# RWKV-7 mixer on one Trainium2 core: four pairs' small products on the array's column tiles, sample states on its four quarters, states loaded at once

## The chip, the cores and the metric

The kernel runs on one core of one Trainium2 chip. The metric is the device time of one execution in microseconds (us); before the change the median of three runs is 1444.45 us (1440.34 to 1446.25). The engines are named as in the profile: PE is TensorE's matrix products, DVE is VectorE, ACT is ScalarE, POOL is GpSimd, SP is SyncE.

## The reference

Two layers of a trunk for a prompt of 256 tokens and eight samples of four new tokens each, 288 columns in all, with D_MODEL 1024. Each layer is a half-step SwiGLU FFN, a mixer, and a second FFN, each after an RMSNorm with shift, scale and gate from a conditioning vector. The mixer is RWKV-7 (8 heads of 64) beside causal pooling; the change is in the RWKV part alone.

```
def _wkv_step(S, inp):
    r_t, w_t, k_t, v_t, a_t, b_t = inp
    sa = jnp.einsum('bhvk,bhk->bhv', S, a_t)
    S = S * w_t[:, :, None, :] + sa[..., None] * b_t[:, :, None, :] + v_t[..., None] * k_t[:, :, None, :]
    y = jnp.einsum('bhvk,bhk->bhv', S, r_t)
    return S, y
...
    kk = kk / jnp.maximum(jnp.sqrt(jnp.sum(kk * kk, axis=-1, keepdims=True)), 1e-12)
    k = hs(k.astype(f32) * (1 + (a - 1) * k_a.astype(f32)))
    S_T, y = lax.scan(_wkv_step, wkv0.astype(f32),
                      (tm(r), tm(decay), tm(k), tm(v), tm(-kk), tm(kk * a)))
    y = ((y - mean) * lax.rsqrt(var + GN_EPS)).reshape(Bn, L, A_WIDTH)
    y = y * ln_w.astype(f32) + ln_b.astype(f32)
    bonus = jnp.sum(r * k * r_k.astype(f32), axis=-1, keepdims=True) * v
    y = (y + bonus.reshape(Bn, L, A_WIDTH)) * g.astype(f32)
```

The samples start from a state of 64 x 64 per head and sample (`state_wkv`, 1 MB per layer), and the new states are outputs.

## The kernel before

Activations lie with channels on the 128 partitions and the 288 tokens in the free dimension. A pair is two heads on one 128-partition tile (`HP` = 4 pairs, index hp or j; e is the head in it). `halves` are partitions 0 to 63 and 64 to 127, `quarter` the four groups of 32.

**Main products.** All large weights come as one stream, a 512 KB tile at a time on SP's queue. For each 128 x 512 strip ACT rounds a high half `wh` (L225), DVE subtracts it for the low half `wl` (L226), and `mm3` (L251) multiplies three times: (wh, xh), (wh, xl), (wl, xh). The "main product" of this text is one such multiplication, 128 x 128 by 288 columns. The halves have four buffers, the raw tiles three.

**The mixer** (L610) interleaves two streams on PE. `main_ops` is a generator of the mixer's main products (input projections, gates, pool branch). The other stream is the RWKV part, small fp32 products written out in order. `add` puts small items into `queue`, each followed by `WEAVE` = 2 steps of `main_ops`; `fill(n)` pops n entries, with n from the table `PLAN` where none is given. So the order of the instructions on each engine is fixed when the program is built, and each engine runs them in that order; only their waits depend on time. PSUM has three banks for main products (`psmm`), four (`pswk`, from `ps_wk`) that all small products share in turn, and one for the modulation (`psmd`).

**The small stream, in order.** Low-rank products (L801) and, for each j, the sum of squares of the keys (L822), four products into four column tiles of one bank; their root; scaled A, R, B, K; the scores MM (L893); a chain of DVE operations that inverts 16 x 16 blocks to GT and, with L1165 to L1197, 64 x 64 blocks; in between the queue's bonus sums (L966) and the transpositions of A and BK (L905). Then the prompt's chunks (L1257, L1262, L1275, `outputs` L1233/L1237, `transposed` L1244), with the samples woven in from the queue: `smp_state` for each pair (L1034 loads the pair's states on ACT's DMA queue, L1037 multiplies them by the rows of A and R, L1040 masks into `ms` and L1041 reduces), `smp_scores`, `smp_rows`, `smp_x`, `smp_u`, `smp_y`, later `smp_last` for each pair (L1136 loads the states again, L1138 makes `uv` on POOL, L1141 multiplies, DVE adds, POOL scales, SP stores). All state tiles of one pair share one buffer, tag "O0". `group_norm` (L1085) takes DVE, ACT and POOL steps (L1092 to L1100) and ends in `yn`, which `transposed` needs; `out_gate` (L1106) makes the output gate, `gated` (L1126) applies it. At the end `yah` (L509) splits the result for the branch product.

## Time and profile before

| what | value |
|---|---|
| median of three runs | 1444.45 us |
| lowest and highest run | 1440.34, 1446.25 us |
| profiled execution's own time | 1440.62 us |
| its span | 1438.8 us |
| mean granted clock of PE | 0.998 |
| mixer of layer 0 in the span, about | 276 to 449 us |
| mixer of layer 1 in the span, about | 988 to 1164 us |

The span runs from the first to the last instruction of the profiled execution; its own time has 1.8 us around it. Times in the rows are microseconds from the span's start. A product in fp32 whose operands are not transposed through the identity is two passes and stands as two instructions in the trace; the count at a row's end is of passes. A bracket at a row's end is idle time before it and what ended it.

### The profile page before, as it was taken

What the parts mean: (1) busy time and instruction counts of PE and PEld (TensorE: products, weight loads), DVE (VectorE), ACT (ScalarE), POOL (GpSimd) and SP (SyncE); (2) the same over time, 40 slices, a digit from 0 to 9 for tenths busy, and PEclk for the clock granted to TensorE, in tenths of its full rate; (3) what the DMA queues carried; (4) which work ended last, traced back from release to release, by engine and by line L of the source; (5) the groups of instructions that cost most, each with busy time, mean ns of one, the idle gap of its engine ahead of it and who ended that gap; (6) DMA issues with size and microseconds to landing.
All of it is one profiled execution on the core that took longest, in us unless ns stands there. A gap on an engine that the chain in (4) does not pass through costs nothing.

```text
span 1438.8 us, 29985 instructions
## 1 busy us (share of the span) xinstructions
PE 1395.2 (97%) x11872; PEld 1292.8 (90%) x11872; DVE 945.0 (66%) x2061; ACT 725.9 (50%) x1477; POOL 110.8 (8%) x155
## 2 busy tenths in 40 slices
PE   6999999998999999999999999999999999999997
PEld 5989999887788999899999999998787899999997
DVE  4655556898766885455667555669967777755554
ACT  4544444675534664444445445447653356545532
POOL 0000001000022010000211000120001200100012
PEclk9999999999999999999999999999999999999999
DMA  9888864443225676787766745553333357445452
GB/s 367 313 283 298 307 242 157 148 134 125 87 94 158 253 251 226 275 302 264 252 226 234 264 147 163 172 179 124 112 105 109 103 188 268 158 152 171 161 169 100
DMA packets 72573, 281.92 MB, mean 196 GB/s; under 512 B 9584, under 2 KB 11760, under 8 KB 63088
## 3 DMA queue, kind: packets, MB, share of 16 engines
q1 hardware_dynamic: 66384, 272.24, 54.6%
q10 hardware_dynamic: 6048, 7.77, 1.8%
q8 instruction: 93, 1.52, 0.4%
q14 instruction: 48, 0.39, 0.1%
HBM read 275.74 MB, written 4.23 MB: 195 GB/s over the span
## 4 chain that ended last, share of the span: by engine, by line
PE 87%; DVE 6%; DMA 2%; issue 2%; ACT 2%; POOL 1%; POOLq 0%; DVEq 0%; ACTq 0%
PE psmm L251 44%; PE pswk L251 31%; PE psmd L315 4%; DVE wl L226 2%; DMA s<-in_wkv 1%; PE pswk L905 1%; PE pswk L1037 1%; PE pswk L393 1%; ACT wh L225 1%; DVE MM L897 1%; DMA o_wkvs<-s 0%; DVE ul L484 0%; DVE xn L481 0%; PE pswk L1262 0%; DMA cc<-in_c 0%
## 5 line engine op out<-in xcount | busy, mean ns | idle before, releaser
L226 DVE TENSOR_TENSOR wl<-raw,wh 128x512 fp32r<-128x512 f32 x732 | 513.7, 704 | 352.3 <-ACT wh L225 341.2
L225 ACT CAST wh<-raw 128x512 fp32r<-128x512 f32 x732 | 452.6, 620 | 563.9 <-PE psmm L251 290.3
L251 PE MATMUL psmm<-uh,wh 128*128 128x288 f32 x1072 | 321.0, 299 | 1.2 <-ACT uh L492 1.2
L251 PE MATMUL psmm<-uh,wl 128*128 128x288 f32 x1072 | 317.8, 296 | 4.5 <-DVE wl L226 4.5
L251 PE MATMUL psmm<-ul,wh 128*128 128x288 f32 x1072 | 317.6, 296 | 0.6 <-DVE ul L493 0.3
L251 PEld LDWEIGHTS psmm<-uh,wh 128*128 128x128 f32 x1072 | 201.9, 188 | 15.8 <-issue 7.7
L251 PEld LDWEIGHTS psmm<-uh,wl 128*128 128x128 f32 x1072 | 201.7, 188 | 8.7 <-DVE wl L226 5.8
L251 PEld LDWEIGHTS psmm<-ul,wh 128*128 128x128 f32 x1072 | 201.8, 188 | 2.6 <-DVE ul L493 1.2
L251 PE MATMUL pswk<-ul,wh 128*128 128x288 f32 x608 | 179.6, 295 | 0.0
L251 PE MATMUL pswk<-uh,wh 128*128 128x288 f32 x608 | 179.4, 295 | 0.0
L251 PE MATMUL pswk<-uh,wl 128*128 128x288 f32 x608 | 179.4, 295 | 0.0
L251 PEld LDWEIGHTS pswk<-uh,wh 128*128 128x128 f32 x608 | 114.5, 188 | 5.4 <-issue 5.0
L251 PEld LDWEIGHTS pswk<-ul,wh 128*128 128x128 f32 x608 | 114.5, 188 | 0.0
L251 PEld LDWEIGHTS pswk<-uh,wl 128*128 128x128 f32 x608 | 114.4, 188 | 0.0
L251 PE MATMUL pswk<-hl,wh 128*128 128x288 f32 x352 | 104.0, 296 | 0.0
L251 PE MATMUL psmm<-hl,wh 128*128 128x288 f32 x352 | 104.0, 295 | 0.0
L251 PE MATMUL psmm<-hh,wh 128*128 128x288 f32 x352 | 103.9, 295 | 0.0
L251 PE MATMUL psmm<-hh,wl 128*128 128x288 f32 x352 | 103.8, 295 | 0.0
L251 PE MATMUL pswk<-hh,wl 128*128 128x288 f32 x352 | 103.8, 295 | 0.0
L251 PE MATMUL pswk<-hh,wh 128*128 128x288 f32 x352 | 103.4, 294 | 0.0
L315 PE MATMUL psmd<-modw,csilu 128*32 128x512 f32 (+2 forms) x832 | 70.5, 481 | 9.4 <-DMA modw<-in_wmod 9.4
L378 POOL TENSOR_TENSOR sq<-x 128x288 f32<-128x288 f32 x28 | 19.8, 707 | 767.1 <-DVE x L520 767.1
(327 smaller groups left out, 2409.7 us busy)
## 6 DMA issues: line engine op xcount, KB each, us to landing
raw<-in_wflat SPq DMA_DIRECT2D x366, 512.0 KB, 3.4
modw<-in_wmod SPq DMA_DIRECT2D x72, 1024.0 KB, 7.0
s<-in_wkv ACTq DMA_DIRECT2D x16, 256.0 KB, 3.0
o_wkvs<-s SPq DMA_DIRECT2D x8, 256.0 KB, 2.9
x<-in_x SPq DMA_DIRECT2D x1, 1152.0 KB, 5.8
o_y<-yo SPq DMA_DIRECT2D x2, 288.0 KB, 2.5
o_y<-yo ACTq DMA_DIRECT2D x2, 288.0 KB, 2.6
o_pool<-po SPq DMA_DIRECT2D x8, 67.5 KB, 2.3
```

The source lines that it names most:

```text
L225: self.nc.scalar.copy(wh, src)
L226: self.nc.vector.tensor_tensor(out=wl, in0=src, in1=wh.bitcast(F32), op=ALU.subtract)
L251: self.last = self.nc.tensor.matmul(ps, w, x, start=start and n == 0, stop=stop and n == 2)
L315: mm = nc.tensor.matmul(self.mod_ps[32 * q:32 * q + 32, :size], self.csilu[:, k, :], w[:, kk, q, :], start=(k == 0), stop=(k == KD - 1))
L378: nc.gpsimd.tensor_tensor(out=t, in0=x, in1=x, op=ALU.mult)
L393: nc.tensor.matmul(ps[:, i:i + 1], s[:, o:o + P], self.cst("ones"), start=n + i == 0, stop=n == len(self.sums) - 1 and i == 2)
L897: V.tensor_tensor(out=MM[:, 2 * e + i, :, q].rearrange("p h x t -> p h (x t)"), in0=pss[e].rearrange("p (h y) -> p h y", h=HP), in1=maskp, ...
L905: T.transpose(ps[:n, 128 * hp:128 * hp + 128], src(hp), ident)
L1037: T.matmul(ps[halves[e], :], ARs[halves[e], hp].rearrange("p x t -> p (x t)"), s0[halves[e]].rearrange("p b v -> p (b v)"), start=True, st ...
```

## The change

Seven edits, all in the mixer but for the last:

- the four key-square products are issued together, after the four squares have been made (`tj` has four buffers)
- the four bonus products likewise, from four `rkk` tiles made ahead; the four transpositions of A become two queue items (`removal`) ahead of the bonus
- states: one tile `s0` for all four pairs, loaded by one DMA at the mixer's start instead of twice for each pair; `smp_state` and `smp_last` take two pairs at a time, one bank for each, and `smp_last` updates `s0` in place and stores two pairs with one DMA
- `at_` places head e of an odd pair in the other half of the output, so that the two pairs' products lie on four quarters of the array
- scores, rows, value rows and yt go into two banks by the parity of the pair, in the same manner
- the queue's items are regrouped: bonus spread and gate for all four tiles at once, lasts in two items (the three lists of the queue have 7 items each instead of 9, 9 and 11)
- the program sets aside less memory for DMA descriptors (`dynamic_dma_scratch_size`), which leaves room for `s0`

```
         def tj(name):
-            return tl([P, NT], "tj", name, bufs=3)
+            return tl([P, NT], "tj", name, bufs=4)
...
         kps = self.ps_wk()
+        kks = []
         for j in range(HP):
             lora_mm(j)
-            t = tl([P, NT], "tj", "kk2", bufs=3)
-            S.activation(out=t, in_=xk[:, j, :], func=AF.Square, scale=self.par(l, "k_k", j))
-            T.matmul(kps[32 * j:32 * j + 32, :NT], hs, t, start=True, stop=True)
+            kks.append(tj("kk2"))
+            S.activation(out=kks[j], in_=xk[:, j, :], func=AF.Square, scale=self.par(l, "k_k", j))
+            if j == HP - 1:
+                for i, t in enumerate(kks):
+                    T.matmul(kps[32 * i:32 * i + 32, :NT], hs, t, start=True, stop=True)
             fill()
...
+        add(lambda: removal(0), lambda: removal(1))
         add(lambda: bonus())
-        add(*[lambda i=i, q=q: token_major(lambda hp: A[:, hp, 2 * i + q, :], AT[halves[q], i, :]) for i in range(2)
-              for q in range(2)])
         add(*[lambda i=i, q=q: token_major(lambda hp: BK[:, hp, i, 2 * q:2 * q + 2, :], BKT[i][:, q, :])
...
-        def rkk(j):
-            t = tj("rkk")
-            V.tensor_tensor(out=t, in0=xr[:, j, :], in1=xk[:, j, :], op=ALU.mult)
-            return t
+        def removal(i):
+            for q in range(2):
+                token_major(lambda hp: A[:, hp, 2 * i + q, :], AT[halves[q], i, :])
+        rkk = [tj("rkk") for _ in range(HP)]
+        for j in range(HP):
+            V.tensor_tensor(out=rkk[j], in0=xr[:, j, :], in1=xk[:, j, :], op=ALU.mult)
...
             for j in range(HP):
-                T.matmul(ps[32 * j:32 * j + 32, :NT], rks[:, j, :], rkk(j), start=True, stop=True)
+                T.matmul(ps[32 * j:32 * j + 32, :NT], rks[:, j, :], rkk[j], start=True, stop=True)
             S.copy(bsum, ps[:, :NT])
...
         bm = self.cst("bmask").unsqueeze(2).to_broadcast([P, NB, 64])
+        s0 = tl([P, HP, NB, 64], "s0")
+        nc.scalar.dma_start(out=s0, in_=self.io["wkv"][l])
         head_loop = [(hp, e) for hp in range(HP) for e in range(2)]
+        def at_(hp, e):
+            return (e + hp) % 2
         def smp_scores():
-            ps = self.ps_wk()
+            pss = [self.ps_wk() for _ in range(2)]
             for hp, e in head_loop:
-                re = halves[e]
-                T.matmul(ps[re, 64 * hp:64 * hp + 64], BKs[re, hp].rearrange("p x t -> p (x t)"),
+                re, o = halves[e], 64 * (hp // 2)
+                T.matmul(pss[hp % 2][halves[at_(hp, e)], o:o + 64], BKs[re, hp].rearrange("p x t -> p (x t)"),
                          ARs[re, hp].rearrange("p x t -> p (x t)"), start=True, stop=True)
-            masks = self.cst("masks").rearrange("p (x t) -> p x t", x=2).unsqueeze(1).to_broadcast([P, HP, 2, NS])
-            V.tensor_tensor(out=SCs, in0=ps[:, 0:256].rearrange("p (h x t) -> p h x t", h=HP, x=2), in1=masks,
-                            op=ALU.mult)
+            masks = self.cst("masks").rearrange("p (x t) -> p x t", x=2).unsqueeze(1).to_broadcast([P, 2, 2, NS])
+            for k in range(2):
+                V.tensor_tensor(out=SCs[:, k::2], in0=pss[k][:, 0:128].rearrange("p (h x t) -> p h x t", h=2, x=2),
+                                in1=masks, op=ALU.mult)
             G.tensor_copy(Gs, self.cst("id32").unsqueeze(1).to_broadcast([P, HP, NS]))
...
-            ps = self.ps_wk()
+            pss = [self.ps_wk() for _ in range(2)]
             for hp, e in head_loop:
-                re = halves[e]
-                T.matmul(ps[re, 64 * hp:64 * hp + 64], BKs[re, hp].rearrange("p x t -> p (x t)"), ident[re, re],
-                         start=True, stop=True)
-            S.copy(BKTs, ps[:, 0:256].rearrange("p (h k) -> p h k", h=HP))
-            ps = self.ps_wk()
+                re, o = halves[e], 64 * (hp // 2)
+                T.matmul(pss[hp % 2][halves[at_(hp, e)], o:o + 64], BKs[re, hp].rearrange("p x t -> p (x t)"),
+                         ident[re, re], start=True, stop=True)
+            for k in range(2):
+                S.copy(BKTs[:, k::2], pss[k][:, 0:128].rearrange("p (h k) -> p h k", h=2))
+            pss = [self.ps_wk() for _ in range(2)]
             for hp, e in head_loop:
-                T.matmul(ps[quarter[2 * e + 1], 64 * hp:64 * hp + 64], xv[halves[e], hp, TP:],
+                o = 64 * (hp // 2)
+                T.matmul(pss[hp % 2][quarter[2 * at_(hp, e) + 1], o:o + 64], xv[halves[e], hp, TP:],
                          ident[halves[e], halves[e]], start=True, stop=True)
-            for e in range(2):
-                r = quarter[2 * e + 1]
-                S.copy(UVs[r], ps[r, 0:256].rearrange("p (h k) -> p h k", h=HP))
-        def smp_state(hp):
-            s0 = tl([P, NB, 64], "O0", "s0")
-            nc.scalar.dma_start(out=s0, in_=self.io["wkv"][l][:, hp])
-            ps = self.ps_wk()
-            for e in range(2):
-                T.matmul(ps[halves[e], :], ARs[halves[e], hp].rearrange("p x t -> p (x t)"),
-                         s0[halves[e]].rearrange("p b v -> p (b v)"), start=True, stop=True)
-            ms = tl([P, NB, 64], "ms")
-            V.tensor_tensor(out=ms, in0=ps.rearrange("p (b v) -> p b v", b=NB), in1=bm, op=ALU.mult)
-            V.tensor_reduce(out=AS[:, hp, :], in_=ms.rearrange("p b v -> p v b"), axis=AX.X, op=ALU.add)
+            for k in range(2):
+                for e in range(2):
+                    r = quarter[2 * e + 1]
+                    S.copy(UVs[r, k::2], pss[k][r, 0:128].rearrange("p (h k) -> p h k", h=2))
+        def smp_state(hps):
+            pss = [self.ps_wk() for _ in hps]
+            for hp, ps in zip(hps, pss):
+                for e in range(2):
+                    T.matmul(ps[halves[at_(hp, e)], :], ARs[halves[e], hp].rearrange("p x t -> p (x t)"),
+                             s0[halves[e], hp].rearrange("p b v -> p (b v)"), start=True, stop=True)
+            for hp, ps in zip(hps, pss):
+                ms = tl([P, NB, 64], "ms", bufs=2)
+                V.tensor_tensor(out=ms, in0=ps.rearrange("p (b v) -> p b v", b=NB), in1=bm, op=ALU.mult)
+                V.tensor_reduce(out=AS[:, hp, :], in_=ms.rearrange("p b v -> p v b"), axis=AX.X, op=ALU.add)
...
         def smp_yt():
-            ps = self.ps_wk()
+            pss = [self.ps_wk() for _ in range(2)]
             for hp, e in head_loop:
-                r = quarter[e]
-                T.matmul(ps[halves[e], 32 * hp:32 * hp + 32], yn[2][r, 64 * hp:64 * hp + 64], ident[r, r],
+                r, o = quarter[at_(hp, e)], 32 * (hp // 2)
+                T.matmul(pss[hp % 2][halves[e], o:o + 32], yn[2][r, 64 * hp:64 * hp + 64], ident[r, r],
                          start=True, stop=True)
-            gated(slice(TP, NT), ps[:, 0:32 * HP])
+            for k in range(2):
+                gated(slice(TP, NT), pss[k][:, 0:64], slice(k, HP, 2))
...
-            y = ps.rearrange("p (h t) -> p h t", h=js.stop - js.start)
-            tmp = tl([P, 512], "pw", "ygw", bufs=2)[:, :ps.shape[1]].rearrange("p (h t) -> p h t", h=js.stop - js.start)
+            n = len(range(HP)[js])
+            y = ps.rearrange("p (h t) -> p h t", h=n)
+            tmp = tl([P, 512], "pw", "ygw", bufs=2)[:, :ps.shape[1]].rearrange("p (h t) -> p h t", h=n)
             V.tensor_tensor(out=tmp, in0=y, in1=out[1][:, js, t], op=ALU.mult)
...
-        def smp_last(hp):
-            s0 = tl([P, NB, 64], "O0", "s0")
-            nc.scalar.dma_start(out=s0, in_=self.io["wkv"][l][:, hp])
-            uv = tl([P, NB, 64], "ms", "uv")
-            G.tensor_tensor(out=uv, in0=UVs[:, hp, :].unsqueeze(1).to_broadcast([P, NB, 64]), in1=bm, op=ALU.mult)
-            ps = self.ps_wk()
-            for e in range(2):
-                T.matmul(ps[halves[e], :], BKTs[halves[e], hp, :], uv[halves[e]].rearrange("p b v -> p (b v)"),
-                         start=True, stop=True)
-            V.tensor_tensor(out=s0, in0=s0, in1=ps.rearrange("p (b v) -> p b v", b=NB), op=ALU.add)
-            G.tensor_tensor(out=s0, in0=s0, in1=gam[:, hp, NCH:].unsqueeze(2).to_broadcast([P, NB, 64]), op=ALU.mult)
-            nc.sync.dma_start(out=self.io["o_wkvs"][l][:, hp], in_=s0)
-        def state(hp):
-            return lambda: smp_state(hp)
-        def last(hp):
-            return lambda: smp_last(hp)
+        def smp_last(hps):
+            uvs = [tl([P, NB, 64], "ms", "uv", bufs=2) for _ in hps]
+            pss = [self.ps_wk() for _ in hps]
+            for hp, uv in zip(hps, uvs):
+                G.tensor_tensor(out=uv, in0=UVs[:, hp, :].unsqueeze(1).to_broadcast([P, NB, 64]), in1=bm, op=ALU.mult)
+            for hp, uv, ps in zip(hps, uvs, pss):
+                for e in range(2):
+                    r = halves[at_(hp, e)]
+                    T.matmul(ps[halves[e], :], BKTs[r, hp, :], uv[r].rearrange("p b v -> p (b v)"),
+                             start=True, stop=True)
+            for hp, ps in zip(hps, pss):
+                s1 = s0[:, hp]
+                V.tensor_tensor(out=s1, in0=s1, in1=ps.rearrange("p (b v) -> p b v", b=NB), op=ALU.add)
+                G.tensor_tensor(out=s1, in0=s1, in1=gam[:, hp, NCH:].unsqueeze(2).to_broadcast([P, NB, 64]), op=ALU.mult)
+            h0, h1 = hps[0], hps[-1] + 1
+            nc.sync.dma_start(out=self.io["o_wkvs"][l][:, h0:h1], in_=s0[:, h0:h1])
...
             fill(1)
-        add(state(0), state(1), smp_scores, state(2), smp_rows, state(3), smp_x, smp_u, smp_y)
+        add(lambda: smp_state((0, 1)), smp_scores, smp_rows, lambda: smp_state((2, 3)), smp_x, smp_u, smp_y)
...
             if c == 1:
-                add(*[lambda js=js: spread_bonus(js) for js in ((0, 1), (2, 3))],
-                    *[lambda js=js: out_gate(js) for js in ((0, 1), (2, 3))],
-                    lambda: outputs(0), last(0), smp_yt, lambda: transposed(0), last(1), last(2), last(3))
+                add(lambda: spread_bonus(range(HP)), lambda: out_gate(range(HP)), lambda: outputs(0), smp_yt,
+                    lambda: transposed(0), lambda: smp_last((0, 1)), lambda: smp_last((2, 3)))
         V.tensor_tensor(out=Sfin, in0=Sfin, in1=gam[:, :, NCH - 1:NCH].to_broadcast([P, HP, 64]), op=ALU.mult)
...
     arrays = pack(inputs)
-    nc = bacc.Bacc("TRN2", target_bir_lowering=False, num_devices=1)
+    nc = bacc.Bacc("TRN2", target_bir_lowering=False, num_devices=1, dynamic_dma_scratch_size=1024)
     io = {}
```

How it stands on the engines. PE, layer 0, around the second state block before (`s` are state tiles, `ARs`, `BKs` the sample rows):

```order
L251 MATMUL psmm<-uh,wh_4733 128x288
L251 MATMUL psmm<-ul,wh_4733 128x288
L1037 MATMUL pswk<-s_4703,ARs 64x512 x2
L251 MATMUL psmm<-uh,wl_4734 128x288
L999 MATMUL pswk<-ARs,BKs 64x64 x8
L251 MATMUL psmm<-uh,wh_4772 128x288
```

and the same place after, where L1054 is the state product, L1013 the scores and L1035 the rows:

```order
L1275 MATMUL pswk<-X_4493,MM 64x64 x16
L1054 MATMUL pswk<-s_4017,ARs 64x512 x4
L1013 MATMUL pswk<-ARs,BKs 64x64 x8
L251 MATMUL psmm<-ul,wh_4742 128x288
L251 MATMUL psmm<-uh,wl_4743 128x288
L251 MATMUL psmm<-uh,wh_4742 128x288
L251 MATMUL psmm<-ul,wh_4742 128x288
L251 MATMUL psmm<-uh,wl_4743 128x288
L251 MATMUL psmm<-uh,wh_4742 128x288
L1035 MATMUL pswk<-consts,BKs 64x64 x8
```

The scores now follow a block of four state products with no main product between; before, a block of two stood among main products.

DVE, layer 0, from the first masked state product on, before (`pw`, `dd` are the pooling's tiles, `SCs` the scores):

```order
L1040 TENSOR_TENSOR ms<-pswk,consts 128x512
L1041 TENSOR_REDUCE AS<-ms 128x64
L226 TENSOR_TENSOR wl_4853<-raw_4597,wh_4852 128x512
L675 TENSOR_TENSOR pw<-px 128x422
L675 TENSOR_TENSOR pw<-pw 128x420
L675 TENSOR_TENSOR pw<-pw 128x416
L1040 TENSOR_TENSOR ms<-pswk,consts 128x512
L678 SCALAR_TENSOR_TENSOR dd<-pw,px 128x256
L684 SCALAR_TENSOR_TENSOR dd<-pw,px 128x32
L1041 TENSOR_REDUCE AS<-ms 128x64
L681 TENSOR_TENSOR dd<-pw,consts 128x16
L1002 TENSOR_TENSOR SCs<-pswk,consts 128x256
```

and after, where L1058 and L1059 are the mask and the reduction, L1017 evicts the scores:

```order
L1058 TENSOR_TENSOR ms<-pswk,consts 128x512
L1059 TENSOR_REDUCE AS<-ms 128x64
L1058 TENSOR_TENSOR ms<-pswk,consts 128x512
L1017 TENSOR_TENSOR SCs<-pswk,consts 128x2x64
L1059 TENSOR_REDUCE AS<-ms 128x64
L1017 TENSOR_TENSOR SCs<-pswk,consts 128x2x64
L1023 STREAM_SHUFFLE shs_4682<-SCs 128x128
L1026 TENSOR_TENSOR shs_4682<-shs_4682,Gs 128x32x3
L1028 TENSOR_TENSOR Gs<-Gs,shs_4682 128x32x3
L1023 STREAM_SHUFFLE shs_4686<-SCs 128x128
L675 TENSOR_TENSOR pw<-px 128x422
L1026 TENSOR_TENSOR shs_4686<-shs_4686,Gs 128x32x2
```

Two state pairs' operations now stand together, and no weight half (`wl`) among them until much further on.

ACT, layer 0, at the mixer's end before (`yah` is the rounded result, `gA` a gate):

```order
L225 CAST wh_5545<-raw_5428 128x512
L1136 DMA s_5412<-in_wkv 128x512
L509 CAST yah<-xv 128x288
L765 ACTIVATE gA_5453<-psmm,par_84 128x288
L225 CAST wh_5561<-raw_5428 128x512
L509 CAST yah<-xv 128x288 x2
L225 CAST wh_5583<-raw_5491 128x512
L509 CAST yah<-xv 128x288
```

and after:

```order
L1115 ACTIVATE ysq_5365<-yn_5361 128x512
L225 CAST wh_5484<-raw_5309 128x512
L225 CAST wh_5506<-raw_5410 128x512
L225 CAST wh_5522<-raw_5410 128x512
L509 CAST yah<-xv 128x288 x4
L225 CAST wh_5544<-raw_5450 128x512
L225 CAST wh_5560<-raw_5450 128x512
L765 ACTIVATE gA_5465<-psmm,par_84 128x288
```

The load of a state tile that stood ahead of `yah` is gone.

## Rows read from the trace of the kernel before

**Rows 1.** The busy table of the whole span.

```profile
PE 1395.2 (97%) x11872; PEld 1292.8 (90%) x11872; DVE 945.0 (66%) x2061; ACT 725.9 (50%) x1477; POOL 110.8 (8%) x155
```

**Rows 2.** Stretches of layer 0's mixer: length, busy by engine, clock, DMA.

```profile
276.00:355.00 79.00, 72.80 (x532) 63.43 (x530) 76.79 (x228) 55.94 (x127) 1.15 (x3) 1.00 0.39 122
328.00:355.00 27.00, 24.39 (x168) 21.10 (x167) 25.74 (x96) 18.32 (x40) 1.15 (x3) 1.00 0.36 112
355.00:441.00 86.00, 83.49 (x1204) 66.88 (x1205) 58.34 (x129) 33.21 (x70) 17.28 (x19) 1.00 0.29 94
```

**Rows 3.** PE's waits, 282 to 450: in total, times, longest.

```profile
PE pswk L893 <- DVE AR L875: 1.6, 1, 1.6
PE pswk L1037 <- DMA s<-in_wkv: 1.6, 1, 1.6
PE psmm L251 <- DVE wl L226: 1.6, 1, 1.6
...
PE pswk L1165 <- DVE dd L681: 1.1, 1, 1.1
```

**Rows 4.** PE's timeline, column tiles and a state pair: start, duration, instruction.

```profile
102.13 3.64 PE L315 MATMUL psmd<-modw,csilu 128*32 128x512 f32 x32
...
381.17 1.08 PE L1037 MATMUL pswk<-s,ARs 64*64 64x512 f32 x4 [1.57 <-DMA s<-in_wkv]
382.18 0.69 PE L1275 MATMUL pswk<-UV,BKT 128*64 128x64 f32 x16
```

**Rows 5.** PE's timeline around a last and yt.

```profile
421.09 1.07 PE L1141 MATMUL pswk<-uv,BKTs 64*64 64x512 f32 x4
422.10 0.40 PE L251 MATMUL psmm<-ybh,wh 128*128 128x288 f32 x1
422.34 0.30 PE L251 MATMUL psmm<-ybl,wh 128*128 128x288 f32 x1
422.47 0.29 PE L251 MATMUL psmm<-ybh,wl 128*128 128x288 f32 x1
...
423.89 0.65 PE L1078 MATMUL pswk<-consts,yn 32*64 32x32 f32 x16
```

**Rows 6.** PE's timeline, transpositions of BK and of yn.

```profile
363.10 1.09 PE L905 MATMUL pswk<-consts,BK 128*128 128x128 f32 x8
...
429.17 0.66 PE L1244 MATMUL pswk<-consts,yn 128*128 128x128 f32 x4
```

**Rows 7.** DVE's groups, 355 to 441: count, busy, mean ns, idle before.

```profile
L226 DVE TENSOR_TENSOR wl<-raw,wh 128x512 fp32r<-128x512 f32 x22 | 15.6, 710 | 5.1 <-ACT wh L225 3.3 <-ACT O L1188 1.4
L1041 DVE TENSOR_REDUCE AS<-ms 128x64 f32<-128x512 f32 x4 | 4.3, 1066 | 0.0
...
L1040 DVE TENSOR_TENSOR ms<-pswk,consts 128x512 f32<-128x512 f32 x4 | 2.8, 688 | 0.8 <-PE pswk L1037 0.8
```

**Rows 8.** DVE's timeline, neighbours and two group norms.

```profile
380.67 0.68 DVE L226 TENSOR_TENSOR wl<-raw,wh 128x512 fp32r<-128x512 f32 x1
381.27 0.25 DVE L1011 TENSOR_TENSOR shs<-shs,Gs 128x96 f32<-128x96 f32 x1
...
419.41 0.69 DVE L1092 TENSOR_REDUCE gn<-pswk 128x8 f32<-128x512 f32 x1 [0.75 <-PE pswk L1237]
...
426.37 0.69 DVE L1100 TENSOR_TENSOR yn<-yn,gn 128x512 f32<-128x512 f32 x1 [1.49 <-POOL gn L1099]
...
436.11 1.52 DVE L1100 TENSOR_TENSOR yn<-yn,gn 128x512 f32<-128x512 f32 x1 [1.53 <-POOL gn L1099]
```

**Rows 9.** Timeline of POOL and ACT near the mixer's end.

```profile
432.91 1.05 POOL L1138 TENSOR_TENSOR uv<-UVs,consts 128x512 f32<-128x512 f32 x1 [6.57 <-PE pswk L1141]
...
444.56 0.33 ACTq L1136 DMA_DIRECT2D s<-in_wkv  x1
444.94 0.43 ACT L509 CAST yah<-xv 128x288 fp32r<-128x288 f32 x1 [4.38 <-DMA o_wkvs<-s]
```

**Rows 10.** DMA issues of the states: count, size, us to landing.

```profile
s<-in_wkv ACTq DMA_DIRECT2D x16, 256.0 KB, 3.0
```

## The prediction, made before the changed kernel was run

> **What bounds the kernel now.** I read the busy table first, then the mixer's stages as windows, then PE's waits there, and last the timelines of the operations that change. Over the whole span PE is busy 97% and DVE 66% [rows 1]. The clock is full throughout (the last figures but two of [rows 2] read 1.00), so no term below is a clock term. The change touches only the mixer, once per layer, and the mixer isn't one stage. From its start to the transposition of GT, 276 to 355, DVE is busy 45.05 of 46 us and 25.74 of the last 27, PE less [rows 2]: DVE bounds it, and PE's waits there end in DVE (1.6 on AR, 1.1 on dd) [rows 3]. From 355 to 441 it is the other way: PE is busy 83.49 of 86 us, DVE 58.34 [rows 2]. The two large waits behind that are the state's DMA (1.6) and, at the stage's end, a weight half wl (1.6) [rows 3]. I call these parts the front and the back, and price one layer; the second has the same pattern.
>
> **The front is worth nothing.** Packing the four squared-key products, keeping the four bonus products together and moving the removal transpositions ahead all save PE's time where PE waits for DVE. The order gives DVE the same instructions in layer 0's front as before, so what PE saves it waits. I take 0; bounded by the two rows of [rows 3] on AR and dd, it could be 1.1 either way. The state load, now one of 1 MB instead of four of 256 KB [rows 10], stands at the mixer's start on ACT's queue, ahead of the pool history's; it has 90 us until it is needed, so I take 0.
>
> **What PE saves in the back.** Tiles do run at the same time. A full-width pass of 288 columns takes 0.13 [rows 5], and yet 32 passes of 512 columns on four column tiles took 3.64 us, 0.11 each; the two products of a state pair, on two diagonal quarters (four passes of 512), took 1.01 from start to next, 0.25 each [rows 4]. Row tiles and column tiles on all four quarters at once are not in this trace. The bounds for two pairs on four quarters are therefore 1.01 (all at once, as the rows of [rows 4] suggest for either kind) and 2.02 (two diagonals in turn); I take 1.01.
> - States: four blocks of 1.01 become two, −2.0. Lasts: 421.09 to 422.10 is 1.01 too [rows 5], so −2.0.
> - Half of BK's transpositions (eight, 1.0 [rows 6]) move to the front, where DVE hides them: −1.0.
> - Scores, rows, X, u, y and yt have as many products as before. The one for yt takes 0.65 [rows 5]; four tiles instead of two could halve such a block or leave it. I take −0.4 for all six (0 to −1.9).
> - Bonus spread and gates are two items instead of four. A main product follows another after 0.13, but after a small block the first takes 0.24 [rows 5], so a switch costs about 0.1 on either side, 0.2 together. The order keeps nearly as many switches (26 against 27), so I take −0.2.
> - The wait for the state's DMA goes: −1.57. It is in the stage that PE bounds, and no load is issued there any more.
> - The tail: PE waits 1.57 for wl at 448.60, since ACT stood 4.38 us behind the store of a state tile (the issue of the next load, 444.56, sits in ACT's queue and waits until the shared tile is stored) and made its halves late [rows 3, 9]. With no load there, the casts run through: −1.57. The later wait of the same kind costs PE nothing now.
> Together −8.74.
>
> **What comes back as new waits.** All four wk banks are taken in pairs now, and evictions by DVE and ACT stand between. Each of these is an estimate, bounded below by 0 and above by the rows named.
> - L1228 behind the last inversion product, with less before it: 0.4. The nearest row is the 1.1 of a small product on a DVE result [rows 3].
> - The scores' third product needs a bank. Two hold the new state pair, one the running sum; so it waits until DVE has evicted the first state bank, 0.69 [rows 7] plus some 0.2 of start: 0.9. In the order the scores follow the state block with nothing between.
> - The rows' products need the second bank, behind another ms, one reduction and the scores' eviction, 0.69 + 1.07 + 0.36, against six main products (0.78) and the scores: 0.65 (0 to 1.1).
> - u needs Xs, which stands 32 DVE instructions behind the first ms. Four ms and four reductions are 7.0 [rows 7], two wl 1.4, and the 22 others at the mean of the rest of the back (58.34 of 129, less 4 × 0.69, 4 × 1.07 and 22 × 0.71, is 0.36) 7.9: 16.3. Neighbours overlap by 0.08 (380.67 + 0.68 against 381.27) [rows 8], 2.5 in all, so 13.8. PE has in the same stretch 49 main products (6.4), L693 (0.3), five small blocks of 0.6 (3.0), the state pair (1.0), seven switches (1.4) and the two stalls above (1.55): 13.7. From 0.1 to 2.6; I take 0.5, near the lower end since most of the 32 have a neighbour that is ready, and 1.5 in layer 1, where the order moves four pooling operations and one wl (2.1 of DVE) into the back.
> - The fourth gate product waits for a bank that ACT and DVE clear: 0.85 (0 to 1.1).
> - The second pair of lasts needs two POOL products of 1.05 each [rows 9], 2.1, behind 12 main ones and two switch sides, 1.8: 0.4.
> - transposed(0) waits for the group norm. Its chain took 419.41 to 427.06, 7.7 [rows 8]; PE's cover is yt 0.6, 28 main products 3.7, S times WT and five switch sides, some 5.8. From 0 to 1.9; since other DVE work between shrinks, 0.5.
> - transposed(1) had three lasts and more between. Now 39 main products stand there, 5.3 with its switch; the chain took 429.17 to 437.63, 8.5 [rows 6, 8]. I take 7.2, somewhat under the shorter of the two, since DVE holds less beside it: 1.9 (0 to 3.2).
> Together +6.1, in layer 1 +7.1.
>
> **A rule weighed.** DVE's eviction of a state pair is 0.69 + 1.07 [rows 7] beside a PE block of 1.01 [rows 4]; two pairs bring 3.5 behind 1.0. The Trainium skill ("TensorEngine Tiling (Array Packing)", section Performance Considerations, PSUM Bottleneck) says that tiling speeds up TensorE but not the evacuation of PSUM, which may then be the bottleneck. This trace agrees by those numbers. By the rule taken alone the states' −2.0 would be given back, and the sum above gives back 0.9 + 0.65 + 0.5 of it.
>
> **The sum.** −8.74 + 6.1 = −2.6 in layer 0, −8.74 + 7.1 = −1.6 in layer 1: −4.2. On the profiled execution's 1440.62 us that is 1436.4. The median of the three runs is 1444.45, 3.8 above the profiled execution, so for a median I forecast 1440.
>
> **Rivals.**
> 1. The waits don't appear: DVE's overlaps and the spare time in main products cover them, and PE's saving counts in full. 2 × −8.74 = −17.5: 1427. For it: the back has DVE busy only 58 of 86 us. Against: the order puts no main product between the state pair and the scores.
> 2. Slower: DVE becomes the bound between the state pair and u, and again through the group norm. The place is the list from ms to Xs; without overlap 16.3, plus a start of 0.75 behind PE for each state pair [rows 8], 17.8, against PE's 13.7: 4.1 instead of 0.5. If the group norm's chains come as long as in the trace, 1.9 + 3.1 instead of 0.5 + 1.9: +2.6. So +3.6 + 2.6 = +6.2 per layer, net +3.6 and +4.6: 1453. It decides from the point where the two waits together exceed what I counted by 2.6 us. For: nothing of wl stands in it, so what PE needs next is late as well; against: in the trace DVE is idle a third of this stage.
> 3. It doesn't do what it says: the four quarters go as two diagonals in turn. Then states and lasts stay at 2.0 a pair of pairs, +4.0 per layer, of which some 0.5 returns as cover: 2 × 3.5 − 4.2 = +2.8, 1447. For: two diagonals at once are nowhere in the trace; against: row tiles and column tiles each are [rows 4].
> The rule that speaks for the third: the Trainium skill ("TensorEngine Tiling (Array Packing)", section Restrictions and Gotchas, Gotcha 1) says that different row tiles cannot access one PSUM bank at the same time. The trace differs in the case that it has: both row tiles of a state pair write one bank, and the block takes 1.01 for four passes [rows 4].
>
> **How the numbers follow.** Forecast 0.46, rival 1 0.22, rival 2 0.14, rival 3 0.13, others 0.05. The forecast's own spread is about 5 us, from the bounds of the stalls. The range 1429 to 1450 leaves out the better part of rival 1 (0.12) and most of rival 2. About 0.5% (7.2 us) is what a measurement here can tell from no change. Faster by more (under 1437.2): rival 1 and a quarter of the forecast, 0.33. Slower by more (over 1451.7): two thirds of rival 2, and some of the others, 0.13. Within: 0.54.
>
> **What would show it.** PE in the new trace: the state pair of four products in 1.0 (rival 3: 2.0); a wait of about 0.9 on ms at the scores, and one at u (0.5; rival 2: about 4); no wait on the state's DMA and none on wl behind the last transposition; a wait of 1 to 3 us at the last transposition on yn or its sums. In the front PE's busy time falls and its waits for DVE grow by the same; if the front becomes shorter by over 1 us, my zero there was wrong. The back (transposition of GT to the last transposition) should be 2 to 3 us shorter in layer 0; if it is the same or longer while PE's blocks halve, the stalls were sized too small.

## The result and the profile after

The changed kernel takes 1451.47 us (median of four runs, 1450.96 to 1452.77); the kernel before 1443.22 in the same comparison. The ratio is 1.006 (95% interval 1.004 to 1.0081): slower by 0.6%, where 1440 was forecast and the range ended at 1450. The profiled execution took 1452.77 us, its span is 1451.0.

The page's first part and two rows of its second, after (busy time, share, instructions; then 40 slices of the span, the granted clock and PE's busy share in tenths):

```profile
PE 1398.4 (96%) x11872; PEld 1301.3 (90%) x11872; DVE 945.6 (65%) x2067; ACT 726.7 (50%) x1483; POOL 110.1 (8%) x155
...
PE   6999999898899999999999999999999999999997
...
PEclk9999999989999999999999999998999999999999
```

No engine has much more work than in [rows 1]. New are two slices with an 8 in the clock: they hold the beginnings of the two mixers. I measure a mixer in two pieces on PE's timeline. The front runs from the spreading of the root mean squares (L407) to the first product with GT, the back from there to the first product with yah:

| kernel | front 0 | front 1 | back 0 | back 1 | half clock in both mixers |
|---|---|---|---|---|---|
| before | 86.7 | 86.7 | 112.5 | 111.7 | 0 |
| changed | 96.0 | 89.4 | 111.3 | 111.9 | 30.7 |

The front lost 9.4 and 2.6 us, the back gave 1.3 and took 0.2. Together that is +10.9 of the 12.2 by which the spans differ; 1.1 of the rest lies ahead of layer 0's mixer (its spreading starts at 269.63 instead of 268.48). Each figure is from one profiled execution.

Stretches of layer 0 after (columns as in [rows 2]; the clock is the third figure from the right):

```profile
277.00:366.00 89.00, 80.05 (x579) 70.08 (x580) 79.28 (x233) 58.09 (x134) 1.15 (x3) 0.90 0.34 112
282.00:298.00 16.00, 12.70 (x38) 8.84 (x39) 9.82 (x29) 7.67 (x24) 0.00 (x0) 0.57 0.19 66
366.00:451.00 85.00, 77.86 (x1159) 62.96 (x1146) 59.11 (x131) 31.24 (x69) 20.05 (x21) 0.98 0.25 85
```

In the front DVE is no longer the bound: 79.28 of 89 us, and 9.82 of 16 between 282 and 298, where the clock averages 0.57. PE's waits, layer 0's mixer, after (total, times, longest):

```profile
PE psmm L251 <- DVE wl L226: 4.2, 1, 4.2
PE pswk L896 <- DVE AR L878: 2.0, 1, 2.0
PE pswk L1262 <- DVE yn L1119: 1.7, 1, 1.7
...
PE pswk L1074 <- DVE Xs L1068: 1.1, 1, 1.1
...
PE pswk L1013 <- DVE ms L1058: 0.7, 1, 0.7
PE pswk L1136 <- DVE xv L1142: 0.7, 1, 0.7
...
PE pswk L1064 <- DVE ms L1058: 0.5, 1, 0.5
PE pswk L1228 <- POOL S L1243: 0.5, 1, 0.5
PE pswk L806 <- DVE S L1300: 0.4, 1, 0.4
PE pswk L1262 <- DVE xv L1151: 0.4, 1, 0.4
...
PE pswk L1035 <- DVE ms L1058: 0.2, 1, 0.2
```

Against [rows 3] the wait for the states' DMA and the wait for wl at the mixer's end are gone, as forecast. The first line is new: a wait of 4.2 us for wl in the front. PE's timeline around it:

```profile
280.81 0.29 PE L251 MATMUL psmm<-vl,wh 128*128 128x298 f32 x1
285.30 0.61 PE L251 MATMUL psmm<-vh,wl 128*128 128x298 f32 x1 [4.20 <-DVE wl L226]
285.71 0.45 PE L251 MATMUL psmm<-vh,wh 128*128 128x298 f32 x1
285.96 0.45 PE L251 MATMUL psmm<-vl,wh 128*128 128x298 f32 x1
```

Behind the wait a main product follows another after 0.25 us instead of 0.13 [rows 5]: the granted clock is 0.5, the 1.2 GHz level. It fell at 283.9, still in the wait, and stays there for 13.7 us, to 297.5. In layer 1 there is a wait of 3.5 us at the same place, and from 997.3 on 10.2 us at 1.2 GHz:

```profile
998.20 0.62 PE L251 MATMUL psmm<-vh,wl 128*128 128x298 f32 x1 [3.47 <-DVE wl L226]
```

What held up wl is read backwards on DVE and ACT. DVE, after:

```profile
283.35 0.87 DVE L484 SCALAR_TENSOR_TENSOR ul<-xn,mod,uh 128x256 fp32r<-128x256 f32 x2
284.14 0.51 DVE L655 SCALAR_TENSOR_TENSOR xla<-p,par,xla 128x287 f32<-128x287 f32 x1
284.57 0.68 DVE L226 TENSOR_TENSOR wl<-raw,wh 128x512 fp32r<-128x512 f32 x1
```

Its cast wh had ended at 282.25; wl stands in DVE's order behind the low halves ul and the shifted row xla, and these came late. ACT, after:

```profile
269.77 0.34 ACTq L1000 DMA_DIRECT2D s<-in_wkv  x1
...
272.34 0.62 ACT L225 CAST wh<-raw 128x512 fp32r<-128x512 f32 x1 [1.27 <-DVE xn L481]
274.00 0.62 ACT L225 CAST wh<-raw 128x512 fp32r<-128x512 f32 x1 [1.04 <-PE psmm L251]
274.53 0.91 ACT L483 ACTIVATE uh<-xn,mod 128x256 fp32r<-128x256 f32 x2
...
280.07 0.62 ACT L225 CAST wh<-raw 128x512 fp32r<-128x512 f32 x1 [1.25 <-DMA raw<-in_wflat]
...
281.65 0.60 ACT L225 CAST wh<-raw 128x512 fp32r<-128x512 f32 x1
```

and before, the same activation:

```profile
270.46 0.51 ACT L483 ACTIVATE uh<-xn,mod 128x256 fp32r<-128x256 f32 x1 [0.55 <-DVE xn L481]
```

The load stands where the pool history's loads stood, and in the new order two casts come ahead of the first uh; the second waits 1.04 us for a buffer that PE frees. So uh starts 4.1 us later (2.9 against the spreading just ahead of it). A second thing is in the row at 280.07: a cast waits for a weight tile. From issue to landing, the weight tiles of 262 to 292, after and before:

```profile
DMA to landing us min/median/max: 3.1/3.4/8.8
```

```profile
DMA to landing us min/median/max: 3.0/3.4/5.6
```

The tile issued at 271.12 landed at 279.97, behind the 1 MB load (269.77 to 277.35).

The back, where my sum was, went as it was drawn. PE's timeline at the first state pair and at the last transposition, after:

```profile
381.83 1.03 PE L1054 MATMUL pswk<-s,ARs 64*64 64x512 f32 x6
382.69 0.28 PE L1013 MATMUL pswk<-ARs,BKs 64*64 64x64 f32 x4
383.65 0.45 PE L1013 MATMUL pswk<-ARs,BKs 64*64 64x64 f32 x12 [0.68 <-DVE ms L1058]
...
449.90 0.63 PE L1262 MATMUL pswk<-consts,yn 128*128 128x128 f32 x4 [1.69 <-DVE yn L1119]
```

The block's first two passes start at 381.72, so two pairs' states take 0.97 us (381.72 to 382.69), no longer than one pair took in [rows 4]. The four quarters of the array do work at once. With the lasts this holds for the first two pairs only:

```profile
431.25 1.09 PE L1162 MATMUL pswk<-uv,BKTs 64*64 64x512 f32 x8
432.27 0.40 PE L251 MATMUL psmm<-ybh,wh 128*128 128x288 f32 x1
...
434.06 1.72 PE L1162 MATMUL pswk<-uv,BKTs 64*64 64x512 f32 x8
435.72 0.40 PE L251 MATMUL psmm<-ybh,wh 128*128 128x288 f32 x1
```

The first block takes 1.02 us, the second 1.66: its second pair starts at 434.71, when POOL's second uv has ended (434.65). PE was not idle in between, so these 0.65 us stand in no list of waits.

### The profile page after: what moved, and what is told of

The parts are those of the page before. It is cut to its first block, busy times and chain, and to the rows that moved or that the text cites. A ratio compares the mean times of both kernels' runs of the same rounds, so it can differ in the third digit from the quotient of the medians.

```text
span 1451.0 us, 29921 instructions
## 1 busy us (share of the span) xinstructions
PE 1398.4 (96%) x11872; PEld 1301.3 (90%) x11872; DVE 945.6 (65%) x2067; ACT 726.7 (50%) x1483; POOL 110.1 (8%) x155
```

## The experiments

**First: which part costs the front.** Four kernels: the load late; the key-squares interleaved; both; and both with bonus and removal as before. The edits, on the changed kernel:

```
s0late:    gcopy = S.copy(gam[:, :, NCH:], ...)
           with tc.issue_after(gcopy.ins):          # behind it on ACT's queue
               nc.scalar.dma_start(out=s0, in_=self.io["wkv"][l])
kkback:    T.matmul(kps[32 * j:32 * j + 32, :NT], hs, t, ...)   # at once after lora_mm(j), as before
s0late_kkback:  both
frontback:      both, and bonus(), rkk(j), the four transpositions of A as before
```

> The changed kernel with one difference: the 1 MB load of the states is issued behind the copy of gam in the front, some 40 us later, instead of at the mixer's start; the key-square products stay packed. Theory 'load' (the load at the mixer's start holds up a weight tile and shifts what ACT and DVE do, PE idles 4.2 us ahead of the low-rank products and its clock falls to half for 13.7 us): 1438 to 1442, no half-clock stretch in layer 0 between 280 and 300, PE's wait on wl there under 1.5 us. Rival 'packing' (the four key-square products issued together leave PE nothing to bridge the low-rank products with): 1449 to 1453, a half-clock stretch in the front as in the changed kernel.

> The changed kernel with the key-square products interleaved with the low-rank products as in the kernel before; the states' load stays at the mixer's start. Theory 'load': 1448 to 1453, the wait on wl of about 4 us and a half-clock stretch of over 10 us at 285 stay. Rival 'packing': 1438 to 1443, no half-clock stretch there.

> Both: the load late and the key-square products interleaved, the rest as in the changed kernel. Both theories: 1437 to 1442, the front as long as before within 1 us. Against the late load with packed products it gives the packing's own price: theory 'load' within 1.5 us of it, rival 'packing' 8 us or more below it.

> The changed kernel's back alone: the load late, key-square products, bonus and removal transpositions as in the kernel before. If the back is worth what I forecast (-2.6 in layer 0, -1.6 in layer 1): 3 to 5 us below the kernel before. If the back's new waits eat all: within 1.5 us of it. If the back is slower: 3 us or more above it.

| kernel | median | ratio to before (95%) | front 0 | front 1 | back 0 | back 1 | half clock |
|---|---|---|---|---|---|---|---|
| changed | 1451.47 | 1.006 (1.004 to 1.0081) | 96.0 | 89.4 | 111.3 | 111.9 | 30.7 |
| kkback | 1454.3 | 1.008 (1.0058 to 1.0102) | 91.0 | 91.5 | 111.7 | 117.5 | 27.3 |
| s0late | 1444.29 | 1.0012 (1.0001 to 1.0022) | 86.4 | 87.3 | 109.8 | 113.7 | 6.8 |
| s0late_kkback | 1445.8 | 1.0017 (1.0006 to 1.0028) | 87.3 | 87.8 | 110.1 | 113.1 | 6.8 |
| frontback | 1437.85 | 0.9963 (0.9949 to 0.9976) | 86.5 | 86.6 | 109.8 | 109.9 | 0 |

The load decides: with it late the front is within 1.1 us of before whether the products are packed or not; with it early it loses 2.6 to 9.4 us either way. Theory "load" holds in that, and "packing" falls as the cause. But packing is not without a part, and kkback missed the load theory's expectation in two points: it came out 1.3 us above the range, and behind its waits (3.2 and 3.5 us) only 3.4 us of half clock lie in each front, where over 10 were expected and the changed kernel has 13.7 and 10.2. Layer 0's front is 5.0 us shorter by it, layer 1's 2.1 longer; most of its half clock (17.1 of 27.3) lies in layer 1's back. (s0late came out 2 us above the top of what the load theory expected, and s0late_kkback 4: that rest is the next point.) And the back alone, with the front of before, makes the kernel faster by 0.37%, 4.7 us between medians.

**Second: bonus and removal.** Between s0late_kkback and frontback lie 8 us, more than the front explains. One kernel takes only that edit back, with the load late and the key-squares packed; frontback was profiled once more:

```
add(lambda: bonus())                      # instead of removal(0), removal(1), bonus()
add(*[lambda i=i, q=q: token_major(lambda hp: A[:, hp, 2 * i + q, :], AT[halves[q], i, :]) ...])
... rks[:, j, :], rkk(j), ...             # rkk made inside bonus()
```

> The changed kernel with the late load and the bonus products and removal transpositions as before; key-square products packed. If the regrouped bonus and removal cost what lies between the two earlier runs (1445.8 with them, 1437.9 without): 1436 to 1440, and layer 1's back at 109.9 us without a half-clock stretch. If instead the packed key-squares cost something of their own: over 1441.

> The kernel with the front of before and the back of the change, looked at once more for the spread of its profile: 1436 to 1440 and no half-clock stretch in either mixer.

s0late_bonback: 1438.22, ratio 0.9979 (0.9963 to 0.9995), fronts 85.5 and 86.4, backs 110.3 and 111.2. frontback again: 1438.36, no half-clock stretch in a mixer, backs 109.8 and 110.2. So the regrouped bonus and removal cost some 6 us between medians (1444.29 against 1438.22; 4.8 by the two ratios). Against my expectation s0late_bonback has half clock left in its mixers: 3.4 us at 390 in layer 0 and 6.8 at 1093 in layer 1, each behind a wait of 1.1 us for Xs that frontback has too, without such a stretch.

The profiled executions hold only 1.0 of these 6 us (1441.36 against 1440.39): s0late's is the fastest of its ten, s0late_bonback's is 2.2 above its median. The rest is seen in the clock of the other executions. All ten of s0late were granted 0.992 to 0.994 and took 1441.4 to 1447.6; of s0late_bonback's ten, eight had 0.993 to 0.998 and took 1434.6 to 1440.4, and two had 0.990 and 0.991 and took 1444.4 and 1445.1. So most of the difference goes with how long PE runs at the lower clock.

In the mixers of the profiles the larger part is layer 1's back, 113.7 against 111.2 and 109.9. PE there with the regrouping (s0late), 10 us:

```profile
1105.00:1115.00 10.00, 8.02 (x47) 5.17 (x48) 3.79 (x9) 2.80 (x7) 1.23 (x2) 0.89 0.19 61
```

and without it (frontback):

```profile
1105.00:1115.00 10.00, 9.47 (x82) 6.05 (x78) 4.58 (x11) 2.38 (x6) 2.46 (x4) 1.00 0.15 54
```

In s0late PE waits there for the second gate weight (g2b), whose DMA was issued at 1105.6 and landed at 1110.1 (1101.7 and 1104.3 in frontback), and then for a gate's bank; the clock is at half from 1112.8 for 6.8 us:

```profile
1110.15 0.76 PE L1140 MATMUL pswk<-sgl,g2b 32*128 32x288 f32 x6 [1.31 <-DMA g2b<-in_g2b]
1112.04 0.75 PE L1137 MATMUL pswk<-sgl,g2a 128*128 128x288 f32 x2 [0.67 <-DVE xv L1143]
```

The traces of the other kernels tell the two apart. In all eight kernels here in which PE waits 1.3 to 1.7 us for g2b (kkback, s0late, s0late_kkback and, of those below, s0pool, s0sp, s0behind, s0u2, s0pool_r3) a half-clock stretch of 6.8 us, in kkback 10.2, begins 0.5 to 2.6 us after that wait. In the five where it is at most 0.5 (changed, polate, s0pool_d2, s0pool_d3, fill4) none begins there, though the bank's 0.7 is the same. polate's row:

```profile
PE pswk L1143 <- DMA g2b<-in_g2b: 0.5, 1, 0.5
```

So the bank's wait alone doesn't do it. It isn't needed either: in kkback and s0late_kkback the clock fell at 1125.1 and 1112.3, and the bank's wait began at 1126.3 and 1113.0. What brings the clock down there is the wait for g2b, and with the bonus as before no kernel has it.

**Third: transfer or order.** The load early, but on another queue, on ACT's queue behind the pool history, or held back on POOL's queue; and the pool history late with no large transfer beside it:

```
s0pool:     nc.gpsimd.dma_start(out=s0, ...)
s0sp:       nc.sync.dma_start(out=s0, ...)
s0behind:   with tc.issue_after(uact[0].ins): nc.scalar.dma_start(out=s0, ...)
s0u2:       with tc.issue_after(uact[2].ins): nc.scalar.dma_start(out=s0, ...)
polate:     s0late, and with tc.issue_after(wsc[1].ins): nc.scalar.dma_start(out=po[:, 1:, :], ...)
s0pool_r3:  G.tensor_copy(s0[:, 0, 0, 0:3], self.r3); nc.gpsimd.dma_start(out=s0, ...)
s0pool_d2, s0pool_d3: as r3, with two or three 128 x 512 products on POOL between
```

> The changed kernel with the states' load at the mixer's start as there, but issued on POOL's queue; PE's order is then that of the kernel with the late load, and ACT's and DVE's front too. Theory 'transfer' (1 MB beside the weight tiles holds one up, and this alone idles PE): 1449 to 1453, front of layer 0 over 93 us. Theory 'order' (the load on ACT's queue moves what stands behind it there: the pool history, the shifted rows, and by them the low-rank products): 1442 to 1446, front of layer 0 within 1.5 us of the late load's 86.4.

> As the run on POOL's queue, but the load stands in SP's queue among the weight tiles, so that the next weight tile can't start before it is issued. Theory 'transfer': 1449 or more, a wait on a weight tile in the front. Theory 'order': 1442 to 1446, front of layer 0 within 2 us of 86.4.

> The changed kernel, the load on ACT's queue a little later: behind the two pool-history loads and two uh activations, so that it starts at some 272 us, 2 us after it does in the changed kernel. The transfer still lies beside the weight tile issued at 271. Theory 'transfer at that moment' (the tile issued at 271 lands at 280 and PE idles): 1448 or more, front of layer 0 over 91 us. Theory 'order' (in the changed kernel ACT has casts that wait for buffers ahead of the uh activations, and the pool history behind the load): 1441 to 1446, front of layer 0 within 2 us of 86.4.

> As the last, but the load still later on ACT's queue (behind the third uh, some 274 us), where the low-rank products come 20 main products earlier on PE than with the late load. Theory 'transfer at that moment': 1446 to 1450, a smaller wait than in the changed kernel since the tile issued at 271 is ahead of it by 3 us. Theory 'order': it depends on the low-rank products' place: if early products idle PE by themselves, front of layer 0 over 90 us; if it is ACT's casts, within 2 us of 86.4.

> The kernel with the late load, and the two pool-history loads moved back on ACT's queue to where they land at some 280 us, as in the changed kernel, with no large transfer beside them. Theory 'transfer': front of layer 0 within 2 us of 86.4 and 1442 to 1446. Theory 'order' through the pool history: front over 90 us and 1447 or more.

> The changed kernel with the load on POOL's queue behind a small copy of the root of the mean squares, so that it starts at some 269.5 us, just ahead of the weight tile issued at 271, while PE's, ACT's and DVE's fronts are ordered as with the late load. Theory 'transfer' : that tile lands at 279 to 280, PE waits 3 us or more for a weight half, front of layer 0 over 90 us, 1448 or more. Theory 'order': the tile lands late as well, but the front of layer 0 stays within 2 us of 86.4 and the time at 1441 to 1446.

> The load on POOL's queue behind two extra POOL operations (their result is overwritten), starting at some 269 us. Theory 'transfer': the weight tile issued at 271 lands at 279 or later, PE waits 3 us or more for a weight half, front of layer 0 over 90 us. Theory 'order': front within 2 us of 86.4, time 1441 to 1446.

> The same with three such operations, starting at some 270 us, 1 us ahead of the weight tile as in the changed kernel. Theory 'transfer': that tile lands at 280, PE waits 3 us or more, a half-clock stretch follows, front of layer 0 over 92 us, 1448 or more. Theory 'order': front within 2 us of 86.4 though the tile lands late, time 1441 to 1446.

| kernel | load issued | tile issued at 271 to 272 lands | front 0 | median | ratio (95%) |
|---|---|---|---|---|---|
| changed | 269.8 | 280.0 | 96.0 | 1451.47 | 1.006 (1.004 to 1.0081) |
| s0late | 306.1 | 276.2 | 86.4 | 1444.29 | 1.0012 (1.0001 to 1.0022) |
| s0pool | 263.9 | 277.7 | 86.5 | 1443.26 | 1.0005 (0.9993 to 1.0016) |
| s0sp | 261.9 | 275.8 | 86.6 | 1441.61 | 0.9991 (0.9979 to 1.0003) |
| s0behind | 272.3 | 276.1 | 87.6 | 1445.12 | 1.0016 (1.0005 to 1.0027) |
| s0u2 | 274.3 | 276.7 | 86.5 | 1443.82 | 1.0009 (0.9989 to 1.0028) |
| polate | 307.4 | 276.6 | 86.1 | 1437.79 | 0.9964 (0.9943 to 0.9984) |
| s0pool_r3 | 267.2 | 277.4 | 87.5 | 1442.8 | 1.0007 (0.9995 to 1.002) |
| s0pool_d2 | 269.5 | 278.4 | 89.1 | 1446.12 | 1.0019 (0.9995 to 1.0043) |
| s0pool_d3 | 270.9 | 279.5 | 87.3 | 1444.58 | 1.001 (0.9996 to 1.0024) |

All fronts are well below the changed kernel's, 86.1 to 89.1. In s0pool_r3 the load started 2.3 us earlier than it was meant to; d2 and d3 come nearer. d2 fits neither theory (front 89.1, but a wait of 1.9 and not 3). The last row comes nearest to the case: the transfer starts 1.1 us later than in the changed kernel and the tile lands 0.5 us earlier, while ACT's front is in the order of the late load. Its tiles, its first uh, PE's wait from 275 to 295 and the stretch after:

```profile
DMA to landing us min/median/max: 3.2/3.3/7.8
```

```profile
272.14 0.51 ACT L483 ACTIVATE uh<-xn,mod 128x256 fp32r<-128x256 f32 x1 [0.67 <-DVE xn L481]
```

```profile
PE psmm L251 <- DVE wl L226: 1.3, 1, 1.3
```

```profile
282.00:298.00 16.00, 15.89 (x107) 12.74 (x107) 15.79 (x47) 14.22 (x40) 0.00 (x0) 1.00 0.46 144
```

PE waits 1.3 us instead of 4.2; the clock stays at full, and the front is 0.9 longer than with the late load. In s0pool_d2 the wait was 1.9 and 3.4 us of half clock followed; its front lost 2.6 (in an execution 2.9 us above its median). So with this order the transfer takes 1 to 3 us of layer 0's front; the rest of the 9.4 comes with the order that the load on ACT's queue brings. That is ACT's order and PE's: from the spreading on, 79 main products stand ahead of the low-rank ones in the changed kernel and 98 in d3. In s0u2 it is 78, and its front loses nothing, so their place alone does not do it. ACT's order without the transfer was not run. In layer 1 d2 and d3 lost more in the front (90.6 and 89.4) than the late load (87.3); there, in these profiles, the transfer alone is enough for the changed kernel's 89.4, though the tile took 8.3 us in d3 and 7.2 in the changed kernel. polate shows that a late pool history by itself costs nothing. It was faster than I expected, in layer 1's front (84.1) and without a half-clock stretch in layer 1's back, where its wait for g2b is short.

**Fourth: the clock.** Filler products where PE waits in the changed kernel:

```
if self.wpos - 1 in (568, 2032) and n == 2:      # in mm3, ahead of the waiting product
    t = self.p_md.tile([P, 512], F32, tag="md", name="idle")
    for k in range(8):
        self.last = self.nc.tensor.matmul(t, self.cst("ident"), self.consts[:, 0:512], ...)
```

> The changed kernel with eight products of a constant tile by 512 columns on PE (their result is not used) at the point where PE waits 4.2 and 3.5 us for a weight half in the two layers. Theory 'clock' (the half clock after the wait costs more than the wait): no half-clock stretch at 285 and 995, front of layer 0 shorter by 5 us or more than the changed kernel's 96.0, total 1442 to 1447. Rival 'wait' (the late weight half and what stands behind it cost the time at any clock): front within 2 us of 96.0, total 1449 to 1453.

1446.74, ratio 1.0028 (1.0017 to 1.0039), fronts 88.9 and 90.4. The filler took longer than the wait:

```profile
281.76 7.03 PE L254 MATMUL idle<-consts 128*128 128x512 f32 x16
288.23 0.70 PE L256 MATMUL psmm<-vh,wl 128*128 128x298 f32 x1
```

The product behind it started 2.3 us later than in the changed kernel, counted from the spreading. Even so the front of layer 0 is 7.1 us shorter. The same stretch with the filler:

```profile
282.00:298.00 16.00, 15.73 (x75) 10.39 (x74) 15.70 (x45) 11.40 (x32) 0.00 (x0) 1.00 0.25 72
```

Clock at full, DVE at 15.70 instead of 9.82. So in layer 0 the half clock, not the wait, was the greater part of the loss. In layer 1 the filler gained nothing (90.4 against 89.4, with 2.8 us of filler beyond the wait, so the full clock gave back 1.8 at most). A reason that fits, not shown by a run of its own, is that the half clock there lay beside DVE's work: DVE is busy 11.76 of the 13 us from 995 in the changed kernel, against 9.82 of 16 in layer 0. The filler also changed the order of a few small products behind it, so 7.1 is not the clock's price alone.

**Fifth: can the gains be added, and what is the scores' wait worth.** The late pool history with bonus and removal as before, and, on frontback, `add(smp_scores, lambda: smp_state((0, 1)), smp_rows, ...)`:

> The kernel with the late load and the pool history later, and bonus and removal as before. If the gains of the two add up: 1433 to 1436. If they are the same gain (no half-clock stretch in layer 1's back): 1437 to 1439.

> The kernel with the front of before and the back of the change, with the scores' item ahead of the first state pair instead of behind it. The scores then need no bank that a state pair holds. By my term for that wait (0.9, and 0.65 for the rows behind it) 1.5 to 3 us below the 1437.9 of that kernel; if u waits for DVE as much longer: within 1 us of it.

1438.72 (0.9975, 0.9965 to 0.9985) and 1438.14 (0.9969, 0.9957 to 0.9981): neither gains on frontback's 1437.85. polate and bonback win the same thing: with either, the long wait for g2b is gone. The scores' place isn't worth anything there, but that doesn't test my term: frontback has no wait at the scores or the rows, only 0.3 at the value rows, which goes. PE's wait for Xs at u stays at 1.1.

## Why the prediction was wrong

The step that failed is "The front is worth nothing", and in it the sentence on the load: "it has 90 us until it is needed, so I take 0". I priced the load by when its data is wanted. What counted is what stands beside it and behind it when it is issued: a weight tile that landed 3.7 us later (279.97 against 276.23 in s0late), and an order on ACT that put two casts ahead of the first uh. In place of 0, the front of layer 0 took 9.4 us, that of layer 1 2.6; with the load late it is 86.4 and 87.3 against 86.7 and 86.7, and the median 7.2 lower. The same step put bonus and removal at 0, too. With the load late they cost 6.1 us between medians, and not in the front: with them regrouped PE waits in layer 1's back for g2b, and half clock follows. (In the changed kernel's own trace that wait doesn't show, so the two prices are not two terms of its 8.2 us.) My bound of 1.1 either way came from waits that were in the trace, for edits whose worst case was a wait that was not.

The Trainium skill says in "DMA: Bandwidth & Descriptors", section Issuing engines are not separate DMA queues, that transfers started by different engines run on the same 16 DMA engines and interleave. This trace agrees: the tile on SP's queue took 8.8 us beside the load on ACT's, and at most 5.6 in the same stretch of the kernel before.

The second failure is that the clock was no term. I read 1.00 in [rows 2] and left it out; but the longest wait there is 1.6 us [rows 3], and behind longer ones the mixers of the changed kernel ran 30.7 us at the lower level. fill4 gave 7.1 us back by keeping PE busy. The Trainium skill ("TensorE: Matmul & The Clock Gate", section HAM oscillation) describes a kernel that does this at every wait for a transfer, and puts the price at half of the throttled time. For 13.7 us that would be an estimate of 6.8, and for layer 1's 10.2 us one of 5.1. fill4's 7.1 is near the first, but it is what was left after 2.3 us of filler beyond the wait; in layer 1 1.8 at most came back.

One reading has its row elsewhere: DVE's 45.05 of 46 us is the stretch 276 to 322, which [rows 2] doesn't show by itself; its first row, 76.79 of 79, says the same.

The steps on the back, one by one for layer 0:
- Four quarters at once: 0.97 for two pairs of states, forecast 1.01, and 1.02 for the first two pairs of lasts. Rival 3 falls.
- The two waits that were to go are gone.
- New waits, forecast and measured: L1228 0.4 and 0.5; scores 0.9 and 0.7; rows 0.65 and 0.2, with 0.5 more at X that I had not listed; u 0.5 and 1.1; gates 0.85 and 0.7; second pair of lasts 0.4 and 0.65; transposed(0) 0.5 and 0.4; transposed(1) 1.9 and 1.7. The one before the bonus spread (0.4) I missed. Sum 6.1 and 6.7. Single terms are off by up to 0.6, so that the sums are this near is in part luck.
- Net: forecast −2.6 and −1.6. The back of the change without half clock in it is s0late's in layer 0: −2.8. In the changed kernel itself layer 0's back holds 3.4 us of half clock at 400 and gave 1.3; layer 1's, with four pooling operations, one wl and eight main products (1.0 us) moved into it, lost 0.2 where I had −1.6.
- frontback measured −2.7 and −1.8 in the two backs, and 4.7 us between medians. That looks like my 4.2, but it is not the same back: all 16 passes of BK's transpositions are in it (8 in the changed kernel), so my −1.0 for them is not, and neither is what I had moved into layer 1's back. For frontback my terms give −1.6 in each layer, 3.2 together; the rest of the 4.7 is gain that I did not price.

Rival 2 named nearly the time (1453), but by the wrong mechanism: it put 4.1 at u, and u waits 1.1, and the group norms' waits came as in the forecast; that the time is near is luck. Rival 1 falls by the waits above.

Open are two things: what ACT's order alone does in the front, without the transfer beside it; and what the wait for g2b alone is worth, since no run takes it away and leaves the rest (polate has it at 0.5 and is 6.5 us below s0late, but its fronts differ too).

## What to carry to other kernels

A load is not free because its data is wanted late: look at what else is in flight when it is issued, and at what the order of its queue's engine becomes. When PE is the bound, keep waits short; a wait of 4.2 us cost 9.4 here, one of 1.3 us at the same place 0.9. Take a change's parts one at a time: here one part (the back) was worth 4.7 us and two others took 13 together (the load 7.2 with the bonus regrouped, the regrouped bonus 6.1 with the load late).

## What was not expected of the hardware

Two row tiles and two column tiles ran together: 8 passes of 512 columns in 0.97 us, 0.12 each, about what a full-width pass of 288 columns takes. In an idle time of 4.2 us the clock fell, and PE ran at 1.2 GHz for 12.2 us after it although it had work again; behind idle times of 3.2 and 3.5 us in kkback it was 3.4 us each. After 1.3 us alone (s0pool_d3) it stayed at 2.4 GHz, after 1.9 us it once ran 3.4 us at the lower level, and after 1.3 and 0.7 us, 1.2 us apart (s0late), 6.8.
